# Closing stage of a gated linear unit: last tile in four pieces, two of them stored by SyncE, and GpSimd waiting for the landings inside a single closing barrier

## Chip, cores, metric

One core of a Trainium2 chip. The metric is the device time of one execution in microseconds (us), lower is better. Beside it stands the span, the time from the program's first to its last own instruction; the difference of the two is called "time outside the span" here. All quoted runs are with a granted clock of 1.0.

## The reference

```python
# x: (8192, 8192) float32
a, b = np.split(x, 2, axis=-1)
return a * (1 / (1 + np.exp(-b)))
```

268.4 MB are read and 134.2 MB written; each output needs one sigmoid and one multiply.

## The kernel before

32 tiles of 256 rows (two rows per partition) go through two input and two output buffers. SyncE issues the loads, ScalarE applies the sigmoid in place, VectorE multiplies, GpSimd issues the stores. The last tile is cut into eight pieces so that its stores can start early. The parts that the change touches:

```python
        else:                                   # the last tile
            w = half // 4                       # half = 4096
            parts = [
                (slice(r, r + 1), slice(c * w, (c + 1) * w)) for r in range(R) for c in range(4)
            ]
        for k, (r, c) in enumerate(parts):
            b = rows[:, r, 1, c]
            sig = nc.scalar.activation(out=b, in_=b, func=SIG)
            mul = nc.vector.tensor_mul(out=packed[:, r, c], in0=rows[:, r, 0, c], in1=b)
            ...                                 # cut: declared dependencies
            if i == n_tiles - 1:
                cols = slice(r.start * half + c.start, r.start * half + c.stop)
                store = nc.gpsimd.dma_start(out=out_t[i, :, cols], in_=os[i % SLOTS][:, cols])
```

The program ends in a block that the tile framework adds and the kernel before leaves as it is: SyncE waits for all 17 semaphores (sixteen for DMA, one for VectorE); then a first barrier (each engine drains and reports, GpSimd gathers and releases); GpSimd clears the semaphores; then a second barrier. One hand edit is already there: the first load is moved ahead of the opening barrier.

## Time and profile before

| | before |
|---|---|
| time, first three runs | 937.08 us median (936.2 to 937.6) |
| profiled run | 936.53 us, span 934.7, outside the span 1.83 |
| last load lands / last store lands | 913.77 / 932.30 us |
| GpSimd's closing drain ends | 933.93 us |

The time is that of the bytes: in this profile the packets of the two data queues take 66.5% and 33.3% of the 16 DMA engines' time. The end is read in three steps. The windows over the last 35 us show when data stops. The view of the closing line shows which engine's closing instruction lasts longest. The records of single landings in the trace, sixteen per transfer, say how far apart the two are. The prediction shows these lines.

### The profile page before, as it was taken

The numbers are of one execution on the slowest core, as the hardware profiler recorded it, in microseconds if no ns is written. First come the engines' busy times: TensorE is split into PE (matmuls) and PEld (weight loads), VectorE is DVE, ScalarE is ACT, GpSimd is POOL, SyncE is SP. The second block draws the span as 40 slices with busy tenths as digits, with TensorE's granted clock in tenths as the row PEclk, the third lists the DMA queues.
The fourth block names the chain that finished last, engine by engine and source line by source line (L and its number), as shares of the span: only waits on it lengthen the run. The fifth ranks groups of instructions, "written<-read, shape, count | busy, mean of one in ns | idle before, by whom it ended". The sixth has DMA issues, their size and how long they took to land.

```text
span 934.7 us, 286 instructions
## 1 busy us (share of the span) xinstructions
DVE 278.7 (30%) x40; ACT 227.0 (24%) x41; POOL 21.1 (2%) x43
## 2 busy tenths in 40 slices
DVE  0333312333123331233321333213332133331333
ACT  1313331133311333203332023330233302333113
POOL 0000000000000000000000000000000000000001
DMA  9999999999999999999999999999999999999998
GB/s 404 423 429 428 464 409 429 445 428 449 425 450 407 466 407 435 440 426 449 425 450 408 464 407 440 435 426 449 446 429 411 461 407 449 426 426 449 425 428 359
DMA packets 10225, 402.67 MB, mean 431 GB/s; under 512 B 1136, under 2 KB 1136, under 8 KB 2160
## 3 DMA queue, kind: packets, MB, share of 16 engines
q1 hardware_dynamic: 4608, 268.44, 66.5%
q0 software_dynamic: 5616, 134.22, 33.3%
q14 instruction: 1, 0.01, 0.0%
HBM read 268.44 MB, written 134.22 MB: 431 GB/s over the span
## 4 chain that ended last, share of the span: by engine, by line
DMA 72%; DVE 14%; ACT 11%; issue 1%; POOL 0%; POOLq 0%; ACTq 0%
DMA x_sb<-in_x_dram 72%; DVE o_sb L67 14%; ACT x_sb L66 11%; POOL out_dram L79 0%; POOLq L104 0%; ACTq L66 0%; POOLq L79 0%
## 5 line engine op out<-in xcount | busy, mean ns | idle before, releaser
L67 DVE TENSOR_TENSOR o_sb<-x_sb 128x8192 f32<-128x8192 f32 (+2 forms) x40 | 278.7, 6983 | 645.4 <-ACT x_sb L66 645.4
L66 ACT ACTIVATE x_sb<-x_sb 128x8192 f32<-128x8192 f32 (+2 forms) x40 | 225.7, 5661 | 693.7 <-DMA x_sb<-in_x_dram 693.7
L82 POOL DMA_DIRECT2D out_dram<-o_sb x31 | 16.6, 536 | 884.5 <-DVE o_sb L67 884.5
L79 POOL DMA_DIRECT2D out_dram<-o_sb x8 | 4.2, 531 | 19.1 <-DVE o_sb L67 19.1
L66 ACT ACT_TABLE_LOAD x1 | 1.3, 1283 | 0.8 <-PEq L128 0.8
L128 POOL MEMSET const-float32-0.0<- 128x1 f32 x1 | 0.1, 98 | 0.2 <-issue 0.2
L128 POOL MEMSET const-bfloat16-1.0<- 128x1 bf16 x1 | 0.1, 101 | 0.0
L128 POOL MEMSET const-float32-1.0<- 128x1 f32 x1 | 0.1, 98 | 0.0
L128 POOL MEMSET const-uint8-127<- 128x1 uint8 x1 | 0.1, 98 | 0.0
## 6 DMA issues: line engine op xcount, KB each, us to landing
out_dram<-o_sb POOLq DMA_DIRECT2D x31, 4096.0 KB, 38.2
out_dram<-o_sb POOLq DMA_DIRECT2D x8, 512.0 KB, 7.6
x_sb<-in_x_dram SPq DMA_DIRECT2D x32, 42.1
```

The source lines that it names most:

```text
L66: sig = nc.scalar.activation(out=b, in_=b, func=SIG)
L67: mul = nc.vector.tensor_mul(out=packed[:, r, c], in0=rows[:, r, 0, c], in1=b)
L79: store = nc.gpsimd.dma_start(out=out_t[i, :, cols], in_=os[i % SLOTS][:, cols])
L82: now["stores"].append(nc.gpsimd.dma_start(out=out_t[i], in_=os[i % SLOTS]))
L128: nc = _bacc.Bacc("TRN2", target_bir_lowering=False, num_devices=1)
```

## The change

The intent is to shorten what follows the last byte. The last tile goes in four pieces instead of eight. SyncE stores the last two, so that GpSimd is finished with its own stores earlier. GpSimd, not SyncE, waits for all landings, between the gather and the release of the only barrier left.

```diff
-            w = half // 4
+            w = half // 2
             parts = [
-                (slice(r, r + 1), slice(c * w, (c + 1) * w)) for r in range(R) for c in range(4)
+                (slice(r, r + 1), slice(c * w, (c + 1) * w)) for r in range(R) for c in range(2)
             ]
...
-                store = nc.gpsimd.dma_start(out=out_t[i, :, cols], in_=os[i % SLOTS][:, cols])
+                queue = nc.sync if k >= len(parts) - 2 else nc.gpsimd
+                store = queue.dma_start(out=out_t[i, :, cols], in_=os[i % SLOTS][:, cols])
...
+def _one_closing_barrier(nc):
+    block = nc.main_func.blocks[2].instructions
+    waits = block[0]                       # SyncE's drain with all waits
+    pool = [i for i in block if i.engine == POOL]
+    drain1, gather1, release1, reset, clear, drain2, gather2, release2 = pool
+    others = [i for i in block[1:] if i.engine != POOL]
+    arrive_and_leave = others[: len(others) // 2]
...
+    landings = sorted(waits.sync_info.on_wait, key=lambda w: w.id == last)
+    pool_waits = [ ... one GpSimd wait for each of landings ... ]
+    block[:] = arrive_and_leave + [drain1, gather1, *pool_waits, reset, clear, drain2, release1]
```

The early first load is only moved into a function of its own. `last` is the semaphore of SyncE's last store.

## The prediction

The sum came to 932.7 us of span and 935.1 us of time, 2.0 us less than before (0.15 + 1.6 + 0.25). "Reads as if it does" means: as if the drain covered GpSimd's own stores. In the trace of before sixteen packets of one queue and sixteen of the other mostly start in turn, which is the "one packet each" below.

> **What bounds the kernel now.** I read the page from the top and then narrowed down on the end, because the change touches only the last of 32 tiles and what closes the program. First the engine shares, the DMA strip and the queues:

> ```profile
> span 934.7 us, 286 instructions
> DVE 278.7 (30%) x40; ACT 227.0 (24%) x41; POOL 21.1 (2%) x43
> DMA  9999999999999999999999999999999999999998
> ...
> q1 hardware_dynamic: 4608, 268.44, 66.5%
> q0 software_dynamic: 5616, 134.22, 33.3%
> ```

> No compute engine is busy a third of the time; the two queues' packets together fill 99.8% of the 16 DMA engines. So the body is set by bytes: 402.7 MB. In the middle of the run one store and one load begin every 29.0 us in the trace, that is 12.58 MB at 434 GB/s, and 402.7 MB at that rate are 928 us. Only some 6.7 us of the 934.7 us span are anything else: about 1 us before the first packet, and the end. No change to the end can be worth 2% (18.7 us). The chain of waits gives the load 72% with VectorE and ScalarE behind it; that is the buffer ring turning, and the change leaves it alone.

> Then the windows over the end, columns: busy time and count of each engine, clock, DMA share, GB/s.

> ```profile
> core 0: us, DVE busy (x) ACT busy (x) POOL busy (x), PEclk, DMA share, GB/s
> ...
> 913.80:921.50 7.70, 6.62 (x6) 7.68 (x8) 2.66 (x5) 1.00 0.97 417
> 921.50:931.50 10.00, 2.55 (x3) 0.00 (x0) 1.59 (x3) 1.00 1.01 412
> 931.50:932.30 0.80, 0.00 (x0) 0.00 (x0) 0.00 (x0) 1.00 0.07 26
> 932.30:934.70 2.40, 0.00 (x0) 0.00 (x0) 0.00 (x0) 1.00 0.00 0
> ```

> The last load lands at 913.8 us. Until 921.5 the DMA engines still drain tile 30's 4 MB store, and from there to 931.5 the last tile's eight 512 KB pieces. They are full all the time: the last tile's arithmetic (over by 924.1) is hidden behind data already queued. The pieces land every 1.25 us, the last at 932.30. Then 2.4 us in which nothing moves. What fills those is in the view of the closing line L104 and in SyncE's own waits:

> ```profile
> L104 SPq EVENT_SEMAPHORE  x10: 17/28/51558, 872.1 to 934.6; - x10
> L104 POOLq EVENT_SEMAPHORE  x4: 17/17/17, 934.0 to 934.6; - x4
> L104 POOLq DRAIN  x3: 45/101/9608, 924.3 to 934.4; - x3
> L104 SPq DRAIN  x3: 7/7/7, 932.7 to 934.2; - x3
> ...
> L104 POOLq EVENT_SEMAPHORE_RANGE_CLEAR  x1: 136/136/136, 934.3 to 934.3; - x1
> ```

> ```profile
> SPq L104 <- DMA out_dram<-o_sb: 60.3, 2, 51.6
> ```

> The columns are shortest/median/longest in ns, then first and last start. To be seen: GpSimd's first drain starts at 924.32 and lasts 9608 ns, to 933.93, which is 1.63 us after the last landing (932.30). SyncE, which waits for all landings, is through at 932.32, needs six more already satisfied waits at 0.06 us and two drains, and reports at 932.79. So SyncE's report is 1.14 us early: **GpSimd's drain is what ends last**. After it the records run: gather 933.98, release 934.06, reset drain 934.14 to 934.24, clear 934.27 to 934.41, drain 934.44 to 934.49, second gather 934.53, second release 934.61, TensorE's last step to 934.71. From the end of the drain that is 0.78 us.

> [...] about 434 GB/s both where the queues alternate (one packet each) and where GpSimd's runs alone on 32 KB packets. So the SyncE stores give no bandwidth. [...] the 9.6 us drain, ending after the last landing although the last issue ended at 924.88, reads as if it does.

> **The change part by part.**

> 1. Pieces of 2048 columns. From the groups by form, VectorE takes 8692 ns for 8192 elements and 4421 for 4096: 0.15 us plus 1.043 ns an element, so 2.29 us for 2048 (started 0.08 us before the one ahead ends, as now). ScalarE likewise 1.90 us. First sigmoid 913.79 to 915.69, multiplies end at about 918.0, 920.2, 922.4 and 924.6, against 924.05 for the last one now. GpSimd issues 0.3 us after a multiply: 918.3 and 920.5. Its first piece is needed when tile 30's data runs out, about 921.2; 2.9 us of lead. On the path: 0. SyncE issues at 922.4 and 924.6; the run's very first load took 0.99 us from issue to first packet, so it has data by 923.4 and 925.6, while GpSimd's 2 MB last beyond 926. The engines stay full: 0.

> 2. Fewer, larger packets. Eight pieces of 4 KB packets take 1.246 us each; their bytes at 434 GB/s are 1.209 us, so a piece carries 0.037 us of overhead, 0.30 us in all. Whether it is per packet or per piece, halving both gives back 0.15. Last landing 932.30 - 0.15 = **932.15 us**.

> 3. The last two pieces go through SyncE's queue. GpSimd's own two run alone from 921.4 and share from 923.4 [...]. At 427 GB/s (between 421 for 4 KB and 434 for large packets), alone until 923.4 moves 0.86 MB of 2.10, and the rest at half rate takes 5.8 us: they finish at 929.2[...]. Landed by about 929.7. If the drain ends 1.63 us after GpSimd's own last landing, it ends at 931.3 at the latest, 0.8 us before the last landing of all. **The 1.63 us leave the path.**

> 4. The waits move to GpSimd, after its drain and the gather (SyncE and the others arrive by 925). The built program merges 17 waits into eight instructions of two semaphores and one on the reset drain, SyncE's last store in the eighth. At 0.06 to 0.08 us each, seven are through by 931.3 + 0.13 + 0.55 = 932.0: just hidden. The eighth opens at about 932.17, where now SyncE still had 0.47 us to its report, itself hidden behind the drain.

> 5. One barrier. After the last wait: to the reset drain 0.06, drain 0.10, gap and clear 0.17, gap and drain 0.08, gap 0.04, release to TensorE's last step 0.10 us (each as in the records above): 0.55. The second gather is gone; the first release and its waiters are not on this path any more.

> Sum: 932.15 + 0.02 + 0.55 = 932.7 us of span instead of 934.7, that is 2.0 us less: 0.15 from packets, 1.6 from the drain no longer following the last landing, and 0.25 from the barrier (0.78 became 0.55, less 0.02 for waking from the wait). Off the unprofiled median: 937.08 - 2.0 = **935.1 us**, 0.2%.

> **The rivals.**
> (a) GpSimd's drain waits for all DMA traffic, or ends at a fixed delay after the last data whoever issued it. Then it ends at 932.15 + 1.63 = 933.8, and gather, eight waits, reset, clear and release follow it: 0.05 + 0.08 + 0.6 + 0.55 = 1.3, span 935.1, time about 937.4. For it: in the kernel before, all last landings are GpSimd's, so the trace can't tell the two apart. Against: the drain carries no semaphore, and the first tile's stores and loads give no hint of GpSimd watching SyncE's queue. I give it 12%.
> (b) The queues don't interleave evenly or SyncE's stores start late. If GpSimd's pieces finish only with the last of SyncE's, the drain is back on the path, with up to the time of (a). Against: loads and stores alternate one packet each in the whole body. If SyncE's first packets come 2 us later, the engines still have GpSimd's data; nothing changes. 8%.
> (c) GpSimd's first piece comes late [...] (stores in the body begin 10.5 us after their issue, but behind queued loads): a gap of up to 1 us before 922, time about 936. For it: the lead shrinks from 4.8 us (issue 916.4, first packet 921.2) to 2.9. 10%.
> (d) The end is not what the time counts: the unprofiled time is 1.8 us longer than the span of the same run, and if the runtime's own closing work waits for something, part of the gain is hidden. Then 936 to 937.

> **Range and chances.** The three runs before spread 936.2 to 937.6, so a median of few runs can be off by 0.5 by itself. Main line 935.1, the rivals 936 to 937.4, a better end [...] 934.7: 933.9 to 936.6 should hold it 8 times in 10. Within 2% is 918.3 to 955.8; nothing in the end of the program reaches that far: same 0.98.

> **What would show each step.** In the changed profile: the last landing at about 932.15 (step 2), carried by the SyncE queue; GpSimd's closing drain ending near 930 to 931.3, before that landing (step 3); eight GpSimd waits at 0.06 to 0.08 us, the last ending with the landing (step 4); 0.55 us from there to the end (step 5); DMA share at 1.0 from 913.8 to 931.2 (step 1). Wrong if the drain ends 1.6 us after SyncE's last landing, if a gap stands in the DMA strip after 921, or if the span falls and the time doesn't.

## The result

| | before | changed |
|---|---|---|
| time, six runs each | 937.04 us median (936.2 to 938.78) | 936.07 us median (935.29 to 936.43) |
| ratio, 95% interval | | 0.9988 (0.9975 to 1.0001) |
| profiled run: time, span, outside | 936.53, 934.7, 1.83 | 936.43, 933.8, 2.63 |

A ratio here is worked out from the fast runs of both kernels in the same rounds, so it is not quite the ratio of the quoted medians. The span of a run is on record to 0.1 us, so a time outside the span is good to about 0.05 us. The change is within 2%, as predicted, and the median lies inside the stated range. But it moved by 1.0 us, not by 2.0, and the interval still touches 1. Where did the other microsecond go?

First the page of the changed kernel:

```profile
span 933.8 us, 259 instructions
...
q1 hardware_dynamic: 4896, 270.53, 67.1%
q0 software_dynamic: 4752, 132.12, 32.8%
```

2.1 MB have moved from GpSimd's queue q0 to SyncE's queue q1, as meant. Then the closing line of the changed kernel (columns as in the prediction: shortest/median/longest in ns, first and last start in us):

```profile
L145 POOLq EVENT_SEMAPHORE  x10: 17/43/43, 929.6 to 933.7; - x10
L145 POOLq DRAIN  x3: 40/101/6852, 922.7 to 933.7; - x3
...
L145 SPq DRAIN  x1: 128/128/128, 927.3 to 927.3; - x1
L145 POOLq EVENT_SEMAPHORE_RANGE_CLEAR  x1: 136/136/136, 933.5 to 933.5; - x1
```

GpSimd's drain now runs from 922.7 for 6852 ns, to 929.58. That is 1.40 us after GpSimd's own last landing (928.18 in the records) and well before the last landing of all. The first of the eight waits ends at 930.69, because it also waits for SyncE's first store, which landed at 930.63; the next six follow at 0.087 us each; the eighth opens with the last landing at 933.25 and ends at 933.32, and the span ends 0.52 us later. So the closing did what was planned. The last landing did not: 933.25 instead of 932.15. The windows over the end (same columns as in the prediction) show it:

```profile
core 0: us, DVE busy (x) ACT busy (x) POOL busy (x), PEclk, DMA share, GB/s
...
913.80:921.50 7.70, 3.54 (x2) 5.48 (x4) 0.53 (x1) 1.00 0.94 404
921.50:931.50 10.00, 5.36 (x3) 1.83 (x2) 0.53 (x1) 1.00 0.99 409
931.50:932.30 0.80, 0.00 (x0) 0.00 (x0) 0.00 (x0) 1.00 0.40 164
932.30:933.30 1.00, 0.00 (x0) 0.00 (x0) 0.00 (x0) 1.00 0.04 16
```

Between 932.3 and 933.3 the share is 0.04, that is less than one DMA engine of 16 at work on average. The landing records agree: fifteen of the sixteen parts of the last store landed by 932.31, one at 933.25. The records do not name the engine of a landing, so whether the late part is always the same engine's is not shown. Has the change made it late? The chain of waits from the start says when it fell behind. The first fence is of the kernel before, the second of the changed one (start us, duration us, what):

```profile
0.79 43.09 DMA x_sb<-in_x_dram
43.88 0.02 issue
43.90 7.04 ACT x_sb L66
```

```profile
0.79 45.20 DMA x_sb<-in_x_dram
45.99 0.02 issue
46.01 7.04 ACT x_sb L67
```

The second load, in the first 46 us, already ends 2.1 us later in this run: one part of it landed 2.6 us after the median of the sixteen. In the records one part of every later load, to the end, is late by as much (2.5 to 2.6 us), while one part of each store up to tile 29's is early, by 0.9 to 1.1 us. Once the loads are over, one part of the stores is late, by 0.9 to 1.4 us. So what is called "out of step" here is a shift between loads and stores that leaves the last landing 0.94 us behind the other fifteen; why it doesn't go away is not shown. It begins 870 us before the first changed instruction. The six timed runs of the changed kernel have spans of 933.8, 933.5, 933.8, 933.3, 932.7 and 933.4 us; the best is the 932.7 that was predicted. The text below calls a run "in step" when no part lags (the expectations speak of DMA engines in step; the records show parts, not engines); of a timed run without a kept trace only the span tells, and a long span can have another cause.

The second thing stands in the table: the time outside the span rose from 1.83 to 2.63 us, and it is 2.59 to 2.63 in all six runs of the changed kernel. What follows the span is called the runtime's closing here. In the trace it shows as semaphore updates; among those of semaphore 2, measured from the end of the span, a step that takes 0.10 us in the kernel before, from 1.74 to 1.83, takes 0.51 us in the changed one, from 1.73 to 2.24.

### The profile page after: what moved, and what is told of

Same layout as the page of the kernel before. It is cut to its first block, busy times and chain, and to the rows that moved or that the text cites. A ratio compares the mean times of both kernels' runs of the same rounds, so it can differ in the third digit from the quotient of the medians.

```text
span 933.8 us, 259 instructions
## 1 busy us (share of the span) xinstructions
DVE 278.4 (30%) x36; ACT 226.6 (24%) x37; POOL 17.9 (2%) x37
## 2 busy tenths in 40 slices
DMA  9999999999999999999999999999999999999998
## 3 DMA queue, kind: packets, MB, share of 16 engines
HBM read 268.44 MB, written 134.22 MB: 431 GB/s over the span
## 4 chain that ended last, share of the span: by engine, by line
DMA 73%; DVE 15%; ACT 12%; DVEq 0%; issue 0%; ACTq 0%
DMA x_sb<-in_x_dram 73%; DVE o_sb L68 15%; ACT x_sb L67 12%; DVEq L145 0%; ACTq L67 0%
## 5 line engine op out<-in xcount | busy, mean ns | idle before, releaser
L84 POOL DMA_DIRECT2D out_dram<-o_sb x31 | 16.7, 537 | 886.5 <-DVE o_sb L68 886.5
L81 POOL DMA_DIRECT2D out_dram<-o_sb x2 | 1.1, 533 | 18.6 <-DVE o_sb L68 18.6
```

What stands on the lines that cost most here:

```text
L81: store = queue.dma_start(out=out_t[i, :, cols], in_=os[i % SLOTS][:, cols])
L84: now["stores"].append(nc.gpsimd.dma_start(out=out_t[i], in_=os[i % SLOTS]))
```

## The experiments

Theory after the result: the steps inside the span hold, and the lost microsecond is time outside the span plus one of the sixteen parts of each transfer out of step. Two candidates for the time outside were SyncE's late stores and the single barrier. A third came from the "instruction" queue q14. The trace of the kernel before has two fetches of 8 KB of instructions 1.19 and 1.28 us after the end of the span. In the changed kernel, where ScalarE and VectorE each have six instructions fewer (57 and 58 instead of 63 and 64 in the built program; the trace records two fewer on each: four sigmoids or multiplies are gone, and two barrier instructions), they are not seen by the end of the trace, 2.36 us after that of the span. The trace does not name the engine that a fetch is for, and no trace shows anything waiting for one; clauses of the recorded expectations that say so are cut, as is an estimate in e11's that rested on no measurement.

Twelve experiments ran, all with correct results, each five times (runs of before: nine in each set); e5 is the changed kernel itself and e12 repeats e6. A set of four shares one chip and the runs of before.

| run | pieces, who stores the last two, closing, extra waits | time | before | ratio (95%) | span | outside (range) |
|---|---|---|---|---|---|---|
| e1 | 4, GpSimd, old | 936.29 | 936.54 | 0.9992 (0.9979 to 1.0006) | 934.4 | 1.94 (1.89 to 2.43) |
| e2 | 4, SyncE, old | 936.02 | 936.54 | 0.9990 (0.9978 to 1.0003) | 933.6 | 2.42 (2.16 to 2.45) |
| e3 | 8, GpSimd, single | 937.21 | 936.54 | 1.0004 (0.9991 to 1.0017) | 935.4 | 2.10 (1.98 to 2.11) |
| e4 | changed, + all engines | 934.51 | 936.54 | 0.9978 (0.9965 to 0.9990) | 933.5 | 1.80 (1.77 to 1.86) |
| e5 | changed | 935.93 | 937.14 | 0.9986 (0.9974 to 0.9999) | 933.7 | 2.60 (2.55 to 2.63) |
| e6 | changed, + ScalarE, VectorE | 934.47 | 937.14 | 0.9975 (0.9962 to 0.9989) | 932.6 | 1.87 (1.82 to 1.89) |
| e7 | changed, + the other three | 935.79 | 937.14 | 0.9988 (0.9976 to 1.0001) | 932.6 | 2.57 (2.50 to 2.60) |
| e8 | changed, + 30 on ScalarE, VectorE | 934.79 | 937.14 | 0.9977 (0.9965 to 0.9990) | 933.8 | 1.81 (1.78 to 1.85) |
| e9 | as e1, + ScalarE, VectorE | 936.73 | 936.51 | 1.0001 (0.9989 to 1.0014) | 934.5 | 1.83 (1.79 to 1.88) |
| e10 | as e2, + ScalarE, VectorE | 935.82 | 936.51 | 0.9992 (0.9980 to 1.0005) | 933.7 | 2.12 (2.03 to 2.21) |
| e11 | as e6, all four by SyncE | 934.82 | 936.51 | 0.9983 (0.9969 to 0.9997) | 933.0 | 1.88 (1.86 to 1.92) |
| e12 | as e6 | 934.63 | 936.51 | 0.9979 (0.9967 to 0.9992) | 932.6 | 1.90 (1.83 to 1.93) |

Times are medians in us. The span is that of the one run whose trace is kept; the time outside is the median of the five runs, with their range. In the 27 runs of before it is 1.78 to 1.87.

**First set: the parts one by one, and the instruction counts.**

e1, four pieces only. Edit against the changed kernel:

```diff
-                queue = nc.sync if k >= len(parts) - 2 else nc.gpsimd
+                queue = nc.gpsimd
...
-    _one_closing_barrier(nc)
```

> Four pieces of 2048 columns, all stored by GpSimd, the old two closing barriers. Main theory: only the packet overhead is halved, so the last landing comes 0.15 us earlier and GpSimd's drain still follows it by about 1.63 us: span 934.55 against 934.7 when all DMA engines are in step, one about 0.9 us longer when one is out of step as in the profile of the changed kernel. Rival (the pieces themselves make an engine late): the last of the 16 landings lags by about 1 us in the profile here and span 935.5. Time outside the span (time minus span of the same run): 1.8 us if it comes from SyncE's late stores or from the single barrier, as neither is here.

The closing line of e1:

```profile
L145 POOLq DRAIN  x3: 45/101/8652, 925.0 to 934.2; - x3
```

The drain ends at 933.65, 1.47 us after the last landing (932.18). The span is 934.4, of 934.55 expected, and no part lags, so the pieces themselves delay nobody. The time outside doesn't settle anything here: it is 2.43 us in the run with the kept trace, although neither SyncE's stores nor the single barrier is there, but 1.89, 1.90, 1.94 and 2.20 in the other four. This kernel has 59 and 60 instructions on ScalarE and VectorE, which left the third candidate to be tried.

e2, SyncE's stores with the old closing. Edit against the changed kernel:

```diff
-    _one_closing_barrier(nc)
```

> Four pieces, the last two stored by SyncE, the old two closing barriers with SyncE waiting for the landings. Main theory: GpSimd's drain ends about 1.5 us after GpSimd's own last landing (928 to 929), before the last landing of all; the path is then the landing (932.15) + SyncE's remaining waits and drains 0.47 to 0.55 + gather to end 0.78, span 933.45, 1.25 us under before, with engines in step. Rival (drain waits for all DMA): drain ends 1.6 us after SyncE's last landing, span 934.55. Time outside the span: 2.6 us if SyncE's late stores are what lengthened it, 1.8 us if the single barrier is.

```profile
L145 SPq EVENT_SEMAPHORE  x10: 17/28/28, 929.5 to 933.5; - x10
L145 POOLq EVENT_SEMAPHORE  x4: 17/17/17, 932.5 to 933.5; - x4
L145 POOLq DRAIN  x3: 39/151/8944, 920.4 to 933.3; - x3
```

The drain runs from 920.4 to 929.34, 1.39 us after GpSimd's own last landing (927.95) and 2.60 us before SyncE's last (931.94). GpSimd's next closing instruction starts at 932.5, 3.2 us after its drain and just after SyncE's first drain at 932.4: it now waits for SyncE's report and not for its own drain. The span is 933.6, of 933.45 expected. Rival (a) of the prediction, a drain that follows all traffic, is out. The time outside is 2.42 in the middle (2.16 to 2.45), with 59 and 60 instructions as in e1 but with SyncE's stores.

e3, the closing alone. Edit against the changed kernel: eight pieces and GpSimd's stores as before, and

```diff
-    last = [i for i in body if i.engine == SP and i.opcode == "DMACopy"][-1].sync_info.on_update[0].id
+    last = [i for i in body if i.engine == POOL and i.opcode == "DMACopy"][-1].sync_info.on_update[0].id
```

> Eight pieces, all stored by GpSimd as before, and the single closing barrier with GpSimd waiting after its drain. Main theory: the drain ends at 933.93 as before, then gather, eight satisfied waits at 0.087 us each, reset, clear, drain and release follow it one after the other: span 935.2, that is 0.5 us MORE than before, so the closing change alone loses. Rival (the second barrier was the cost): span 934.45, 0.25 less. Time outside the span: 2.6 us if the single barrier lengthened it, 1.8 us if SyncE's stores did.

```profile
L145 POOLq EVENT_SEMAPHORE  x10: 17/43/43, 934.1 to 935.3; - x10
L145 POOLq DRAIN  x3: 40/93/9535, 924.6 to 935.2; - x3
```

The drain ends at 934.09, after all landings (932.45), and the waits, all long satisfied, queue up behind it from 934.1. The span is 935.4, 0.7 us more than before (expected: 935.2, 0.5 more); the lowest of the five is 935.0, against 934.6 in the runs of before. So with the drain on the path the single barrier lost 0.7 us; with the drain out of the way it gained 1.1 us of span (e10 to e12, below). Time outside 1.98 to 2.11, with 61 and 62 instructions: the single barrier alone doesn't make it 2.6.

e4, the instruction counts restored. Edit against the changed kernel: satisfied waits go ahead of the barrier, beside the last transfers. Two waits end up in one instruction (the 12 written for ScalarE are six in e6's trace), so twice as many are written.

> The changed kernel with satisfied waits added on every engine ahead of the closing barrier, so that each engine again has as many instructions as in the kernel before (88, 63, 64, 8, 73). They lie beside the last transfers, so the span should be that of the changed kernel: 932.7 with the engines in step, up to 933.8 with one out of step. If the time outside the span grew because the instruction counts moved against the fetches of 8 KB of instructions that the trace shows, it falls from 2.62 back to about 1.8 us and the time to 934.5 to 935.6. If it grew for another reason it stays at 2.6.

Adding instructions made the kernel faster (ratio to before 0.9978, against 0.9988 for the changed kernel). The time outside fell to 1.80 us (1.77 to 1.86), the fetches stand at 1.19 and 1.28 us after the end again, the slow step in the runtime's closing is back at 0.10 us, and the time is 934.51 us against 936.54. The profiled run is out of step from the second load on, like that of the changed kernel; the five times fall into 934.29 to 934.51 and 935.36 to 935.37.

**Second set: which engines' counts.**

e5, the changed kernel unaltered.

> The changed kernel, unaltered, on the chip of the next three runs, as their base line. Time outside the span (time minus span of the profiled run) 2.6 us as in its first six runs. The times should fall into two groups about 0.9 us apart: 935.2 where all DMA engines are in step, 936.0 to 936.4 where at least one is out of step from the second load on. If that split is chance and not a consequence of the change, runs of the kernel before show the same two groups (936.4 and 937.5 or more).

Time outside 2.60, as expected; the times are 935.05 and 935.17, and 935.93 to 936.33. The runs of before in this set don't form two groups; they spread evenly from 936.43 to 937.59 (spans 934.6 to 935.8). In the first set they do: five at 936.40 to 936.54 (spans 934.6 and 934.7) and four at 937.02 to 938.19 (935.2 to 936.4). So long spans occur without the change as well. The profiled run of e5 is out of step too, but its last part falls behind bit by bit, from 0.6 us at the second load to 1.6 us by 538 us.

e6, extra waits on ScalarE and VectorE only (`PADS = {E.Activation: 12, E.DVE: 12}`).

> The changed kernel with six extra satisfied waits on ScalarE and six on VectorE only (63 and 64 instructions, as before). Theory: the time outside the span follows the instruction counts of these two[...]; it falls to about 1.85 us and the time to 934.4 (in step) or 935.3 (out of step). Rival: [...] it stays at 2.6.

e7, extra waits on the other three only (`PADS = {E.PE: 4, E.SP: 14, E.Pool: 12}`).

> The counterpart: extra satisfied waits on TensorE (2), SyncE (7) and GpSimd (6) only. Theory: time outside the span stays at 2.6 us and the time at 935.2 or 936.2. Rival [...]: it falls to about 1.85.

These two decide it. With ScalarE and VectorE filled up the time outside is 1.82 to 1.89, and with the other three filled up it stays at 2.50 to 2.60; both have spans of 932.6 in step. Times 934.47 and 935.79. The closing line of e6:

```profile
L160 POOLq EVENT_SEMAPHORE  x10: 17/43/43, 929.5 to 932.5; - x10
L160 ACTq EVENT_SEMAPHORE  x7: 17/38/38, 924.6 to 932.6; - x7
L160 DVEq EVENT_SEMAPHORE  x7: 21/50/50, 924.6 to 932.6; - x7
L160 POOLq DRAIN  x3: 40/101/9027, 920.4 to 932.5; - x3
```

Six of the seven on ScalarE (ACTq) and on VectorE (DVEq) are the extra ones; they begin at 924.6 and are over by 925.2, when both engines drain and report, four microseconds before GpSimd gathers the reports (929.5). The drain ends at 929.45, 1.40 us after GpSimd's own last landing at 928.05; the last landing of all is at 932.05, the end at 932.63. That is the prediction's closing, term by term.

e8, thirty extra instructions on each of the two (`PADS = {E.Activation: 60, E.DVE: 60}`).

> The changed kernel with thirty extra satisfied waits on each of ScalarE and VectorE, all beside the last transfers (30 at 0.1 us from 926.9 are over by 930). Theory: the two fetches move from 1.2 us after the end to before it[...]: time outside the span 1.85 us or less (1.4 to 1.85), time 934.0 to 934.4 in step. If [...] the waits delay the barrier, the time rises again above 935.

The queue lines of e6 and of e8 (packets, MB, share within the span):

```profile
q14 instruction: 1, 0.01, 0.0%
```

```profile
q14 instruction: 4, 0.02, 0.0%
```

Of e8's four packets one has 24 bytes and stands at the start, and one of 8 KB stands in the last 13 us of the span in every kernel. The other two, at 931.61 and 931.69 us, two microseconds before the end of the span, are taken to be the fetches in question, moved into it. That buys next to nothing: 1.81 us outside instead of 1.87. The time is not lower than that of e6 but 0.3 us higher, and this lies inside the span (933.0 in the middle of five runs against 932.6). The profiled run is out of step (one part of the second load 2.3 us late), so it doesn't show whether the extra waits cost this; the cause of the 0.3 is open.

**Third set: the ledger with equal closing, and the drain.**

e9 and e10 are e1 and e2 with eight waits (four instructions) written for each of ScalarE and VectorE at the head of the closing block, which brings both to 63 and 64.

> The first experiment (four pieces, all stored by GpSimd, old closing) with ScalarE and VectorE filled up to the 63 and 64 instructions of the kernel before, so that all four runs of this set have the same closing work outside the span, about 1.85 us. What is left is the pieces alone: span 934.4 to 934.6 in step, 0.1 to 0.3 us under before; if its gain is only packet overhead the time is 0.1 to 0.4 us under the runs of before.

> The second experiment (last two pieces by SyncE, old closing) filled up in the same way. Theory: span 933.4 to 933.6 in step, outside 1.85, time 935.2 to 935.5 in step: the drain off the path is worth 0.9 to 1.0 us over the run before this one, and the single barrier the remaining 0.9 to 1.0 to the last run of this set. Rival (SyncE's late stores lengthen the closing work by themselves): outside above 2.2 us.

e9 shows that the pieces alone are worth little: span 934.5 (lowest 934.1, against 934.4 in the runs of before), outside 1.83, time 0.2 us above that of before, inside its scatter. In e10 the span is 933.7. Its time outside is 2.12, more than the 1.85 expected and less than the rival's 2.2. So SyncE's stores with the old closing go with 0.3 us more outside, and with 0.5 more from e1 to e2. Its trace has one more 8 KB fetch, 1.89 us after the end, and SyncE has 77 instructions here (73 in the kernel before); e2, with the same 77, has one at 1.84 that e1, with 73, has not. Whether that fetch goes with SyncE's count, and whether it costs this time, was not tried.

e11, all four pieces stored by SyncE. Edit against e6:

```diff
-                queue = nc.sync if k >= len(parts) - 2 else nc.gpsimd
+                queue = nc.sync
```

> The changed kernel with all four pieces stored by SyncE and ScalarE and VectorE filled up. Theory of the drain: it ends 1.4 to 1.6 us after GpSimd's own last landing, which is now tile 30's at about 922.3, so it ends at 923.7 to 923.9 with ten us of data still under way. Rival (it ends with the traffic of all queues or at the end of the data): it ends after 930. Time as the next run, 934.4 in step, as the drain is off the path in both[...].

```profile
L160 POOLq EVENT_SEMAPHORE  x10: 17/43/43, 925.6 to 932.9; - x10
L160 POOLq DRAIN  x3: 40/101/22902, 901.3 to 932.8; - x3
```

The drain starts at 901.3, when GpSimd has issued tile 30's store, and lasts 22.9 us, to 924.23. Tile 30's store landed at 922.91. So the drain ends 1.32 us after GpSimd's own last landing, with 8 us of SyncE's transfers still under way. (The expectation put the landing at 922.3; in this run one part lags by 1 us, which also fits the span of 933.0.) The time is that of e6 and e12 within their scatter.

e12, e6 once more.

> The padded version of the changed kernel again, on another chip: outside the span 1.85 to 1.9 us, time 934.4 in step and 935.3 to 935.6 out of step, about 2.1 us under the kernel before in step and 0.2 to 0.3% in the mean.

934.63 us, 934.3 to 934.8, ratio 0.9979; all five runs lie in the lower group. (It ran on a chip with the same number as in the second set, so it is a repeat and not a second chip; e4, with the same two counts, was on another.)

## Why the prediction was right, and what it missed

- The bound, the size class and the range: right. Nothing at the end was near 2%; the time is 936.07 against 935.1 predicted, inside 933.9 to 936.6. The range held because it was drawn to take in the rivals: the main line's gain of 2.0 us came out as 1.0, with an interval that touches no change, and where the median falls depends in part on how many of the six runs were out of step.
- Step 1, the engines stay full: right for runs in step, where SyncE's data is there before GpSimd's runs out (DMA share 0.98 from 921.5 to 931.5 in e6). In the changed kernel's own profile the last load came at 916.0, GpSimd's first store was issued at 920.5 instead of 918.3, and the share from 913.8 to 921.5 is 0.94 against 0.97 before: a small gap like that of rival (c), but for another reason.
- Step 2, 0.15 us from packets: right in direction, too small to resolve in time. The middle one of the sixteen landings of the last transfer is at 931.75 before and between 931.54 and 931.73 in the in-step profiles of four pieces (e1, e2, e6, e7, e9, e10, e12), so 0.02 to 0.21 us. The last landing is at 931.94 to 932.07 in those with SyncE's stores, against 932.15 predicted.
- Step 3, the drain leaves the path: right, and shown by e2 and e11 against rival (a), which had 12%. One detail was wrong: the queues were to share the engines from 923.4. In e6 SyncE's first packet starts at 926.0, 3.6 us after the issue at 922.4 and when GpSimd's data is nearly through, so the two queues ran one after the other (8 of GpSimd's 256 packets start after SyncE's first). The packet-by-packet alternation that the prediction reads off the body did not carry over to these two. That only helped: GpSimd's last landing was at 928.05, not 929.7. The drain's delay after GpSimd's own last landing was 1.32 to 1.64 us in thirteen of the fourteen profiles. In e4, where extra waits delayed the drain's start to 927.7, it was 2.35 us; why is open.
- Steps 4 and 5, the waits hidden and about 0.55 us to the end: right (0.58 us from the last landing to the end of the span in the changed kernel, e6 and e12). One detail of step 4 was missed: the first of the eight waits is not satisfied beforehand when SyncE's first store lands after the drain (930.63 in the changed kernel, 929.59 in e6), which stayed hidden behind SyncE's second store (landed at 933.25 and 932.05). And the single barrier was given 0.25 us only beside a drain that was credited with 1.6. Moving the stores with the old closing took the span from 934.5 to 933.7 (e9 to e10), and the new closing on to 932.6 (e12): 0.8 and 1.1 us in this order. The second needs the first: by itself the new closing loses 0.7 us (e3). The credit of 1.6 is what the drain costs before; once it is gone, SyncE's remaining waits are the path (in e2 SyncE's last landing is at 931.94, its first drain at 932.4, GpSimd's next step at 932.5), as the prediction's step 4 says without drawing the consequence.
- The sum, span 932.7: right for runs in step (932.6 in e6, e7 and e12, 932.7 in the best run of the changed kernel).
- "Off the unprofiled median: 937.08 - 2.0": **the step that failed**. It takes the time outside the span as constant at 1.8 us. It grew to 2.6. This is rival (d), "if the runtime's own closing work waits for something, part of the gain is hidden", for which it had a time of 936 to 937 but neither a chance nor a mechanism. The cause that e4, e6 and e7 show is the instruction count of ScalarE and VectorE together; which of the two was not separated. At 57 and 58 the time outside is 2.50 to 2.63 in all 16 runs (the changed kernel, e5, e7), at 63 and 64 it is 1.77 to 1.93 in all 25 of e4, e6, e9, e11 and e12. In between the counts don't fix it: 1.89 to 2.45 at 59 and 60 (e1, e2), 1.98 to 2.11 at 61 and 62 (e3); and e10 has 2.03 to 2.21 at 63 and 64. How the counts act is not shown. In the kept traces the fetches after the end of the span move with them: 1.2 to 1.6 us after it at 63 and 64, 1.8 in e3, 2.1 in e1 and e2, not seen at 57 and 58, 2 us before it at 87 and 88. Where the last fetch ends late (2.28 to 2.66 us after the end, in e1, e2, e3 and e10), the time outside is that end less 0.2 to 0.3 us; where none is seen after the end at 57 and 58, the slow step of 0.51 or 0.52 us stands in the runtime's closing. Whether anything waits there for a fetch is not shown.
- The ledger: the median span of the changed kernel's six runs is 933.45. That of before, estimated as its median time of 937.04 less 1.83, is 935.2. So the span fell by 1.8 us, the outside rose by 0.8, and 1.0 is left, which is what the medians show.
- What stays open: why runs fall out of step. It showed in five of eight profiles of kernels with SyncE's stores and the single barrier (the changed kernel, e4, e5, e8, e11) and in none of the six others. In three of the five it begins at the second load, long before any changed instruction runs, so a cause in the changed stage is hard to see; and the long spans of before (up to 936.4) speak against it too; but five of eight against none of six is too uneven to call it chance with confidence.

The shortest times are those of e6: 934.47 and 934.63 us in two sets, 0.2% under before. That is clear of the noise (both intervals end below 1), though still within 2%.

## What to carry to other kernels

Read GpSimd's drain by GpSimd's own transfers: here it ended 1.3 to 1.6 us after its own last landing (2.35 in e4). So give the last stores to another queue, and then look for what is next on the path: here moving the stores gave 0.8 us, and the new closing, which lost 0.7 us by itself, then gave 1.1 more. When a change removes instructions near the end, compare time and span of the same runs: the part that lies outside the program's own instructions can grow and hide part of the gain (0.8 of 1.8 us here). Take it over all runs and not from one trace: e1's ranged from 1.89 to 2.43 us. A few satisfied waits on idle engines, placed beside the last transfers, are a cheap test for that: six on each of ScalarE and VectorE took the time outside from 2.60 (e5) to 1.87 us (e6).
